# A decoder trunk on one core: key projection by groups of k tiles, norms by two split products, and the last output tiles apart

## The chip, the cores and the metric

The kernel runs on one core of a Trainium2 chip. The metric is the device time of one execution in microseconds. TensorE (PE) multiplies, VectorE (DVE), ScalarE (ACT) and GpSimd (POOL) work on vectors, SyncE (SP) issues nearly all DMAs. Each engine works through its own instructions in the order in which they were written.

## The reference

One sequence of 256 positions, width 2048, float32, two layers. Layer 0 mixes by attention, layer 1 by a gated linear recurrence; each ends with a gated MLP. What bears on the change:

```
h   = x * rsqrt(mean(x*x) + EPS) * gain                    # before every block: 4 norms in all
qkv = h @ w_qkv                                            # 32 query heads, 8 key and 8 value heads of 64
q, k = rmsnorm(q, q_gain), rmsnorm(k, k_gain)              # over the 64 values of a head
S   = q k^T / 8, causal window of 128, softmax with a learned sink, then O = P v
x   = x + O @ w_o
u   = causal_dwconv3(h @ w_up); g, v = split(u)            # 2048 -> 2 x 6144
x   = x + (gelu(g) * v) @ w_down                           # 6144 -> 2048
# layer 1: x = x + (scan(...) * gelu(h @ w_in_y)) @ w_out, and the same MLP
```

## The kernel before

Positions lie along the free dimension (256 columns), channels along the 128 partitions: `x[:, k]` is k tile `k` of 16. To keep float32 accuracy at the speed of the fp32r format, each operand is split into a high part (an fp32r copy, ACT) and a low part (the difference, DVE), and a product is the sum of three: high weights by high and by low data, low weights by high data. A *chunk* is one [128 x 2048] block of weights (1 MB). Chunks come in the order of a list (`order`); `dma_next`, `split_hi` and `split_lo` load one, copy its high part and subtract its low part, each through three buffers; `advance` does one step of all three.

The program is written out by hand, engine by engine (`manual_schedule`): an instruction that waits holds up all that stands behind it on its engine. An SP DMA takes one of eight completion semaphores in turn and waits until the transfer that had it before has landed, so at most eight transfers are under way.

In order: (1) the four key chunks (`psk`; the products `pk`). Chunks 0 and 1 go by quarters, as x and the weights arrive; chunks 2 and 3 follow whole. (2) The values `pv`, four chunks. Between the second and the third of them `kv_norm` (L476) sums x*x over the channels with products by a matrix of ones; the squares were added up by `early_stat` (ACT squares, DVE adds). (3) Sixteen query tiles j: `attend` (L662) spreads the scores `S` of tile j-1, its softmax, and the value products `O` of tile j-3 among the projection of tile j. `k_epi` and `k_fin` (L446, L457) normalise the four key tiles: `k_epi` copies, adds and squares, `k_fin` sums the squares by a product with `bones` (`ks`), takes the root and writes the parts `kz` that the scores read. Key tile 0 is done in stage 2, tiles 1 to 3 start behind query tiles 1, 3 and 7. (4) The output projection, the MLP, the recurrence (`px`, `py`, `pr`) and the second MLP.

At the start of four stages (`pu` twice, `px`, `pr`) stands `late_pair` (L290): two chunks together, with k tiles 14 and 15 last, and between them, except for `pr`, the norm's product `norm_pe` (L181) of two float32 products. The last output tiles are `x_epi`'s (L245): two additions and two DMAs out.

Of the kernel before, what the change touches and what calls it, by code (L numbers as in the profile page):

```python
# [19 lines left out]
F32 = mybir.dt.float32  # L20
# [5 lines left out]
P = 128  # L26
# [14 lines left out]
def trunk(ctx, tc, xT, wq, wk, wv, wo, win, wg, wout, wup, wdn, mixg, ffng, kqg, sinks,  # L41
# [19 lines left out]
    sqt = per.tile([P, 2, T], F32, name="sqt")  # L61
# [3 lines left out]
    vt = per.tile([P, T], F32, name="vt")  # L65
    nt = per.tile([P, T], F32, name="nt")
# [7 lines left out]

    gap.tile([P, 16], F32, name="pad")
# [82 lines left out]
    def stat(src, first):  # L158

        if first:  # L160
            pool.tensor_tensor(out=sqa, in0=src, in1=src, op=ALU.mult)  # L161
        else:
            pool.tensor_tensor(out=sqt, in0=src, in1=src, op=ALU.mult)
            pool.tensor_tensor(out=sqa, in0=sqa, in1=sqt, op=ALU.add)
# [125 lines left out]
    def late_pair(ps, rhs, mid=None):  # L290

        parts = [use(), use()]
        for i, (hi, lo) in enumerate(parts):
            mm_hi(ps[:, i], hi, rhs, rng(0, KD - 2))
            mm_lo(ps[:, i], lo, rhs, rng(0, KD - 2), stop=False)
        advance()
        if mid:
            mid()
        for i, (hi, lo) in enumerate(parts):
            mm_hi(ps[:, i], hi, rhs, rng(KD - 2, KD), start=False)  # L300
            mm_lo(ps[:, i], lo, rhs, rng(KD - 2, KD))
        advance()
# [25 lines left out]
    def quarter(i):  # L328
        return slice(i * CH // 4, (i + 1) * CH // 4)

    def part(i):
        return slice(i * CH // 2, (i + 1) * CH // 2)

    act.dma_start(out=x[:, 0:1, :], in_=xT[:, 0:1, :])
    act.dma_start(out=gm, in_=mixg)
    for c in range(3):
        raws[c] = rawp.tile([P, CH], F32, tag="raw", name=f"raw{c}")
        his[c] = hip.tile([P, CH], F32R, tag="hi", name=f"hi{c}")
        los[c] = lop.tile([P, CH], F32R, tag="lo", name=f"lo{c}")
    for i in range(4):  # L340
        nc.sync.dma_start(out=raws[0][:, quarter(i)], in_=order[0][:, quarter(i)])
        for a, b in ((1, 2), (2, 4)) if i == 0 else ((4 * i, 4 * i + 4),):
            nc.sync.dma_start(out=x[:, a:b, :], in_=xT[:, a:b, :])
        nc.sync.dma_start(out=raws[1][:, quarter(i)], in_=order[1][:, quarter(i)])
    for i in range(2):
# [747 lines left out]
```

## Time and profile before

| | |
|---|---|
| device time, median of 3 | 2152.42 us (2151.99 to 2154.63) |
| the profiled execution | 2152.51 us, span 2150.7 us |
| PE busy | 2144.2 us (100%), 17930 products |
| DVE, ACT, POOL busy | 68%, 52%, 7% |
| DMA | 405.80 MB, mean 189 GB/s |

The busy share of PE is not its peak: products overlap in the array and their ends are modelled. What counts is from start to start, and where PE waits with nothing in flight. A row of the timeline gives the start, the time it covers, engine, source line, operation, output from inputs, shape and count; in brackets stands how long the engine was idle before it and what it waited for. Rows of several instructions are runs of the same kind.

### The profile page before, as it was taken

The numbers are of one execution on the slowest core, as the hardware profiler recorded it, in microseconds if no ns is written. First come the engines' busy times: TensorE is split into PE (matmuls) and PEld (weight loads), VectorE is DVE, ScalarE is ACT, GpSimd is POOL, SyncE is SP. The second block draws the span as 40 slices with busy tenths as digits, with TensorE's granted clock in tenths as the row PEclk, the third lists the DMA queues.
The fourth block names the chain that finished last, engine by engine and source line by source line (L and its number), as shares of the span: only waits on it lengthen the run. The fifth ranks groups of instructions, "written<-read, shape, count | busy, mean of one in ns | idle before, by whom it ended". The sixth has DMA issues, their size and how long they took to land.

```text
span 2150.7 us, 40983 instructions
## 1 busy us (share of the span) xinstructions
PE 2144.2 (100%) x17930; PEld 2104.3 (98%) x17930; DVE 1459.9 (68%) x1715; ACT 1125.7 (52%) x1317; POOL 140.4 (7%) x125
## 2 busy tenths in 40 slices
PE   9999999999999999999999999999999999999999
PEld 7999999999999999999999999999999999999999
DVE  6787867777644777766679877777775447777643
ACT  6676555555433555544479874555553335555432
POOL 1233320000000000002200004100000000000000
PEclk9999999999999999999999999999999999999999
DMA  7333555555555555555555546555555555555453
GB/s 267 115 119 119 216 178 209 192 191 194 194 196 192 200 195 192 191 187 196 177 215 217 187 147 214 187 205 194 192 191 189 196 192 201 195 193 191 181 202 138
DMA packets 60803, 405.80 MB, mean 189 GB/s; under 512 B 7504, under 2 KB 9936, under 8 KB 12880
## 3 DMA queue, kind: packets, MB, share of 16 engines
q1 hardware_dynamic: 60336, 403.04, 52.6%
q8 instruction: 140, 2.29, 0.4%
q14 instruction: 39, 0.32, 0.0%
q10 hardware_dynamic: 288, 0.15, 0.0%
HBM read 401.06 MB, written 2.10 MB: 187 GB/s over the span
## 4 chain that ended last, share of the span: by engine, by line
PE 97%; DVE 1%; DMA 1%; ACT 1%; issue 0%; DVEq 0%; ACTq 0%
PE pu L204 29%; PE pu L209 15%; PE pd L204 14%; PE pd L209 7%; PE pu L250 4%; PE pd L250 3%; PE py L204 3%; PE pq L204 2%; PE po L204 2%; PE px L204 2%; PE pr L204 2%; PE py L209 1%; PE po L209 1%; PE pr L250 1%; PE pq L209 1%; PE px L209 1%
## 5 line engine op out<-in xcount | busy, mean ns | idle before, releaser
L126 DVE TENSOR_TENSOR lo<-raw,hi 128x2048 fp32r<-128x2048 f32 (+1 forms) x390 | 863.8, 2215 | 279.6 <-ACT hi L118 278.2
L118 ACT CAST hi<-raw 128x2048 fp32r<-128x2048 f32 x373 | 713.1, 1912 | 576.1 <-PE pd L204 216.0
L204 PE MATMUL pu<-h,hi 128*128 128x256 f32 x5504 | 651.8, 276 | 0.0
L204 PEld LDWEIGHTS pu<-h,hi 128*128 128x128 f32 x5504 | 636.6, 188 | 0.0
L209 PE MATMUL pu<-h,lo 128*128 128x256 f32 x2752 | 339.9, 276 | 0.0
L204 PE MATMUL pd<-g,hi 128*128 128x256 f32 x2688 | 332.0, 276 | 0.0
L209 PEld LDWEIGHTS pu<-h,lo 128*128 128x128 f32 x2752 | 324.7, 188 | 0.0
L204 PEld LDWEIGHTS pd<-g,hi 128*128 128x128 f32 x2688 | 317.1, 188 | 0.0
L788 DVE SCALAR_TENSOR_TENSOR uy<-us,fw,uy 128x255 f32<-128x255 f32 (+1 forms) x384 | 176.5, 480 | 6.8
L209 PE MATMUL pd<-g,lo 128*128 128x256 f32 x1344 | 179.6, 276 | 0.0
L209 PEld LDWEIGHTS pd<-g,lo 128*128 128x128 f32 x1344 | 164.8, 188 | 0.0
L288 DVE TENSOR_TENSOR us<-pu,rb 128x512 f32<-128x512 f32 x86 | 59.5, 692 | 149.5 <-PE pu L209 149.5
L795 ACT CAST g<-us 128x256 fp32r<-128x256 f32 x96 | 39.0, 407 | 230.3 <-DVE us L794 230.3
L785 ACT ACTIVATE uy<-us,fb,fw 128x256 f32<-128x256 f32 x192 | 105.1, 595 | 55.3 <-DVE us L288 52.6
L204 PE MATMUL pq<-h,hi 128*128 128x256 f32 x512 | 73.9, 284 | 0.0
L796 DVE TENSOR_TENSOR g<-us,g 128x256 fp32r<-128x256 f32 x96 | 40.9, 426 | 45.3 <-ACT g L795 45.3
L260 DVE TENSOR_TENSOR x<-pd,x 128x512 f32<-128x512 f32 (+1 forms) x35 | 19.8, 583 | 70.1 <-PE pd L209 70.1
L204 PEld LDWEIGHTS pq<-h,hi 128*128 128x128 f32 x512 | 64.6, 188 | 0.2
L161 POOL TENSOR_TENSOR sqa<-x 128x512 f32<-128x512 f32 x3 | 5.0, 1671 | 891.1 <-DVE x L260 891.1
L250 PE MATMUL pu<-h,hi 128*128 128x512 f32 (+1 forms) x272 | 61.9, 378 | 0.0
L204 PE MATMUL py<-h,hi 128*128 128x256 f32 x512 | 60.6, 276 | 0.0
L204 PEld LDWEIGHTS py<-h,hi 128*128 128x128 f32 x512 | 59.2, 188 | 0.0
(247 smaller groups left out, 2134.2 us busy)
## 6 DMA issues: line engine op xcount, KB each, us to landing
raw<-in_wup SPq DMA_DIRECT2D x192, 1024.0 KB, 4.8
raw<-in_wdn SPq DMA_DIRECT2D x96, 1024.0 KB, 4.9
raw<-in_win SPq DMA_DIRECT2D x32, 1024.0 KB, 4.9
raw<-in_wq SPq DMA_DIRECT2D x16, 1024.0 KB, 4.8
raw<-in_wo SPq DMA_DIRECT2D x16, 1024.0 KB, 4.8
raw<-in_wout SPq DMA_DIRECT2D x16, 1024.0 KB, 4.8
raw<-in_wv SPq DMA_DIRECT2D x4, 1024.0 KB, 6.2
graw<-in_wg SPq DMA_DIRECT2D x8, 512.0 KB, 3.5
```

Of the source, the lines that this page charges most:

```text
L118: act.copy(out=his[c], in_=raws[c])
L126: dve.tensor_tensor(out=los[c][:, part], in0=raws[c][:, part], in1=f(his[c][:, part]), op=ALU.subtract)
L161: pool.tensor_tensor(out=sqa, in0=src, in1=src, op=ALU.mult)
L204: pe.matmul(ps, lhsT=hi[:, off + k * n:off + k * n + P], rhs=rhs[:, xk, part, :], start=start and (k, part) == (ks[0][0], 0), stop=False)
L209: pe.matmul(ps, lhsT=lo[:, off + k * n:off + k * n + P], rhs=rhs[:, xk, 0, :], start=False, stop=stop and k == ks[-1][0])
L250: pe.matmul(ps[:, cols], lhsT=w, rhs=rhs, start=first, stop=stop and last.get(id(ps)) == i)
L260: dve.tensor_tensor(out=xs[:, i], in0=ps[:, i, 0:T], in1=t[:, i] if two else xs[:, i], op=ALU.add)
L288: dve.tensor_tensor(out=s[:, i], in0=ps[:, i, 0:T], in1=rbb[:, i], op=ALU.mult)
L785: act.activation(out=y[:, i, :], in_=s[:, i, :], func=AF.Identity, scale=fw[:, layer, n, 2:3], bias=fb[:, layer, n:n + 1])
L788: dve.scalar_tensor_tensor(out=y[:, i, tap:], in0=s[:, i, 0:T - tap], scalar=fw[:, layer, n, 2 - tap:3 - tap], in1=y[:, i, tap:], op0=ALU. ...
L795: act.copy(out=g[:, m, 0, :], in_=s[:, 0, :])
L796: dve.tensor_tensor(out=g[:, m, 1, :], in0=s[:, 0, :], in1=f(g[:, m, 0, :]), op=ALU.subtract)
```

## The change

- All four key chunks go side by side through five groups of k tiles (2, 2, 4, 4, 4): per group five DMAs, the splits, and 12 products per k tile. The low data has a product of its own (`two_hi`, 256 columns) instead of sharing one of 512 columns. Chunk 3's parts lie for the time in `kz`.
- `early_stat` and `kv_norm` move later: the norm now stands between the third and fourth chunk of `pv`. Key tile 0 is finished behind query tile 0 instead of in stage 2. The square of a key tile moves from `k_epi` into `k_fin`, just ahead of the product that reads it.
- The norm's sum: DVE folds the two halves of the squares, ACT and DVE split the result, and two fp32r products take the place of two float32 ones.
- `late_pair` becomes `first_pair`: chunk by chunk, the norm behind both.
- The last two output tiles have PSUM tiles of their own, and their additions stand apart.
- The sums of q's squares (`pq`) are issued before the third product of the first score tile; the softmax scaling on POOL goes head by head.

```diff
-    def norm_pe(ps):
+    def norm_sum(ps):
+        dve.tensor_tensor(out=sqa[:, 0], in0=sqa[:, 0], in1=sqa[:, 1], op=ALU.add)
+        act.copy(out=sqt[:, 0], in_=sqa[:, 0])
+        dve.tensor_tensor(out=sqt[:, 1], in0=sqa[:, 0], in1=f(sqt[:, 0]), op=ALU.subtract)
         for i in range(2):
-            pe.matmul(ps, lhsT=ones, rhs=sqa[:, i, :], start=i == 0, stop=i == 1)
+            pe.matmul(ps, lhsT=onesr, rhs=sqt[:, i], start=i == 0, stop=i == 1)
...
-    def late_pair(ps, rhs, mid=None):
+    def first_pair(ps, rhs, mid=None):
+        for i in range(2):
+            hi, lo = use()
+            if i == 0:
+                two_hi(ps[:, 0, 0:T], hi, rhs, rng(0, KD - 2), start=True)
+                one_lo(ps[:, 0, 0:T], lo, rhs, rng(0, KD - 2), stop=False)
+                two_hi(ps[:, 0, 0:T], hi, rhs, rng(KD - 2, KD))
+                one_lo(ps[:, 0, 0:T], lo, rhs, rng(KD - 2, KD))
+            else:
+                thirds(ps[:, 1, 0:T], hi, lo, rhs, rng(0, KD), 0, P, True, True)
+                if mid:
+                    mid()
+            advance()
...
+        groups = [(0, 2), (2, 4), (4, 8), (8, 12), (12, 16)]
+        for a, b in groups:
+            for c in range(4):
+                nc.sync.dma_start(out=kraw[c][:, a * P:b * P], in_=order[c][:, a * P:b * P])
+                if c == 0:
+                    a0 = max(a, 1)
+                    nc.sync.dma_start(out=x[:, a0:b, :], in_=xT[:, a0:b, :])
...
+        for a, b in groups:
+            for c in range(4):
+                sl = slice(a * P, b * P)
+                act.copy(out=khi[c][:, sl], in_=kraw[c][:, sl])
+                dve.tensor_tensor(out=klo[c][:, sl], in0=kraw[c][:, sl], in1=f(khi[c][:, sl]), op=ALU.subtract)
+                if c == 0:
+                    for k in range(a, b):
+                        split_x(h, x[:, k, :], gm[:, 0], k)
+            for c in range(4):
+                two_hi(psk[c], khi[c], h, rng(a, b), start=a == 0)
+                one_lo(psk[c], klo[c], h, rng(a, b), stop=b == KD)
...
         def k_fin(p):
...
+            act.activation(out=r, in_=s, func=AF.Square)
+            pe.matmul(pk[:, 0:T], lhsT=bones, rhs=r, start=True, stop=True)
...
-        k_from, k_to = {1: 1, 3: 2, 7: 3}, (2, 5, 9)
+        k_from, k_to = {1: 1, 3: 2, 7: 3}, (0, 2, 5, 9)
...
+                    if last:
+                        tiles[1] = mm.tile([P, 2, 512], F32, tag="mm", name="pdlast")[:, 1]
...
+                        for i in range(2):
+                            xs = x[:, 14 + i]
+                            dve.tensor_tensor(out=xs, in0=tiles[i][:, 0:T], in1=xs, op=ALU.add)
+                            nc.sync.dma_start(out=out[:, 14 + i], in_=xs)
```

How the order of instructions moves, at three places. On ACT, behind query tile 3 (`es2` closes the softmax of tile 2, `qh3` and `qsq3` read the finished tile, `kr2` belongs to key tile 2), before:

```order
L610 ACTIVATE pr2_960,sm2_961<-S2_930,nm2_957,rr2_946 128x128 x2
L610 ACTIVATE pr2_960,sm2_961<-S2_930,nm2_957,rr2_946 128x256 x2
L617 ACTIVATE es2_1000<-es2_1000 128x4
L558 CAST qh3_1028<-pq_3_897 128x256
L559 ACTIVATE qsq3_1027<-pq_3_897 128x256
L172 ACTIVATE kr2_1033<-kv2_1032 128x256
```

and now:

```order
L591 ACTIVATE pr2_1046,sm2_1047<-S2_1016,nm2_1043,rr2_1032 128x128 x2
L591 ACTIVATE pr2_1046,sm2_1047<-S2_1016,nm2_1043,rr2_1032 128x256 x2
L598 ACTIVATE es2_1086<-es2_1086 128x4
L455 ACTIVATE kr2_1111<-vn_80 128x256
L539 CAST qh3_1117<-pq_3_983 128x256
L540 ACTIVATE qsq3_1116<-pq_3_983 128x256
L173 ACTIVATE kr2_1111<-kv2_1121 128x256
```

The square (L455) now stands between the softmax of tile 2 and the copies of query tile 3; PE's `ks2` product, which reads it, stands as before right behind the last product of query tile 3.

On DVE around the norm in the `pv` stage (`lo6`, `lo8` are low parts of chunks 6 and 8), before:

```order
L441 TENSOR_TENSOR sqa_75<-sqa_75,sq5_458 128x512
L441 TENSOR_TENSOR sqa_75<-sqa_75,sq6_461 128x512
L441 TENSOR_TENSOR sqa_75<-sqa_75,sq7_464 128x512
L126 TENSOR_TENSOR lo6_495<-raw6_366,hi6_456 128x2048
L485 TENSOR_SCALAR cb_148<-pn_497 128x256
```

and now:

```order
L127 TENSOR_TENSOR lo8_606<-raw8_488,hi8_604 128x2048
L439 TENSOR_TENSOR sqa_75<-sqa_75,sq6_608 128x512
L439 TENSOR_TENSOR sqa_75<-sqa_75,sq7_611 128x512
L184 TENSOR_TENSOR sqa_75<-sqa_75 128x256
L186 TENSOR_TENSOR sqt_76<-sqa_75,sqt_76 128x256
L477 TENSOR_SCALAR cb_124<-pn_614 128x256
```

The low part of a chunk now stands ahead of the last two additions and of the norm's own split.

On PE at the start of the recurrence (`px0` is the first pair, `pnr` the norm), before:

```order
L192 MATMUL px0_12050<-h_73,hi184_11966 128x512 x14
L198 MATMUL px0_12050<-h_73,lo184_11968 128x256 x14
L192 MATMUL px0_12050<-h_73,hi185_12020 128x512 x14
L198 MATMUL px0_12050<-h_73,lo185_12022 128x256 x14
L183 MATMUL pnr_12113<-sqa_75,ones_79 128x256 x2
L192 MATMUL px0_12050<-h_73,hi184_11966 128x512 x2
L198 MATMUL px0_12050<-h_73,lo184_11968 128x256 x2
```

and now:

```order
L209 MATMUL px0_12171<-h_73,hi184_12087 128x256 x28
L214 MATMUL px0_12171<-h_73,lo184_12089 128x256 x14
L209 MATMUL px0_12171<-h_73,hi184_12087 128x256 x4
L214 MATMUL px0_12171<-h_73,lo184_12089 128x256 x2
L209 MATMUL px0_12171<-h_73,hi185_12141 128x256 x32
L214 MATMUL px0_12171<-h_73,lo185_12143 128x256 x16
L188 MATMUL pnr_12274<-sqt_76,onesr_88 128x256 x2
```

k tiles 14 and 15 are read after 42 products instead of after 56 longer ones, and the norm comes behind the whole pair.

## Rows read from the trace of the kernel before

**Rows 1.** The page, costliest groups: splits of whole chunks (after the bar: busy, mean ns)
```profile
L126 DVE TENSOR_TENSOR lo<-raw,hi 128x2048 fp32r<-128x2048 f32 (+1 forms) x390 | 863.8, 2215 | 279.6 <-ACT hi L118 278.2
L118 ACT CAST hi<-raw 128x2048 fp32r<-128x2048 f32 x373 | 713.1, 1912 | 576.1 <-PE pd L204 216.0
```

**Rows 2.** Windows: busy us (count) by engine, then PEclk, DMA share, GB/s
```profile
10.00:20.00 10.00, 10.00 (x55) 7.91 (x54) 9.32 (x19) 9.22 (x19) 0.00 (x0) 1.00 1.03 376
400.00:500.00 100.00, 100.00 (x885) 100.00 (x884) 69.73 (x82) 52.37 (x56) 0.00 (x0) 1.00 0.55 193
```

**Rows 3.** Timeline, key stage, PE and DVE: start, us covered, instruction, idle before
```profile
6.27 2.07 PE L192 MATMUL pk<-h,hi 128*128 128x512 f32 x4 [0.65 <-DVE h L155]
...
8.99 1.57 PE L192 MATMUL pk<-h,hi 128*128 128x512 f32 x4
...
14.42 1.29 DVE L406 TENSOR_TENSOR lo<-raw,hi 128x512 fp32r<-128x512 f32 x2
...
26.31 3.95 PE L192 MATMUL pk<-h,hi 128*128 128x512 f32 x16 [0.63 <-ACT hi L118]
...
31.91 0.39 PE L524 MATMUL pv<-hi,h 128*128 128x512 f32 x1
```

**Rows 4.** Transfers issued from 0 to 14 us: count, KB each, median us to landing
```profile
x<-in_xT SPq DMA_DIRECT2D x1, 128.0 KB, 3.7
```

**Rows 5.** Timeline around the norm of the value stage
```profile
40.85 2.29 DVE L441 TENSOR_TENSOR sqa<-sqa,sq 128x512 f32<-128x512 f32 x3 [2.81 <-ACT sq L439]
...
43.19 1.13 PE L183 MATMUL pn<-sqa,ones 128*128 128x256 f32 x4
...
44.96 0.48 PE L524 MATMUL pv<-hi,h 128*128 128x512 f32 x1
```

**Rows 6.** Timeline: key tile 0 finished, then query tile 0 and the first scores
```profile
55.27 0.83 ACT L473 CAST kz<-kst 64x256 fp32r<-64x256 f32 x2 [1.99 <-DVE kst L470]
...
63.22 0.42 DVE L560 TENSOR_TENSOR qh<-pq,qh 128x256 fp32r<-128x256 f32 x1 [2.63 <-ACT qsq L559]
63.86 0.28 PE L575 MATMUL S<-kz,qh 128*128 128x256 f32 x1
```

**Rows 7.** Timeline: the `ks` products behind query tiles 1, 3 and 7, with ACT
```profile
69.81 0.20 ACT L617 ACTIVATE es<-es 128x4 f32<-128x4 f32 x1
69.83 0.59 PE L460 MATMUL ks<-kst,bones 128*128 128x256 f32 x2
...
87.33 0.59 PE L460 MATMUL ks<-sqt,bones 128*128 128x256 f32 x2
89.02 0.21 ACT L617 ACTIVATE es<-es 128x4 f32<-128x4 f32 x1
...
125.08 0.59 PE L460 MATMUL ks<-nt,bones 128*128 128x256 f32 x2
125.68 0.20 ACT L617 ACTIVATE es<-es 128x4 f32<-128x4 f32 x1
```

**Rows 8.** Timeline, PE: the q sums of query tiles 3 to 6, one per tile
```profile
91.17 0.50 PE L580 MATMUL S<-bones,qsq 128*128 128x2 f32 x4
100.98 0.50 PE L580 MATMUL S<-bones,qsq 128*128 128x2 f32 x4
109.98 0.50 PE L580 MATMUL S<-bones,qsq 128*128 128x2 f32 x4
119.38 0.50 PE L580 MATMUL S<-bones,qsq 128*128 128x2 f32 x4
```

**Rows 9.** Timeline, recurrence: first pair, a split behind it, and the next chunk
```profile
1077.37 3.37 PE L192 MATMUL px<-h,hi 128*128 128x512 f32 x14
...
1081.10 2.27 DVE L126 TENSOR_TENSOR lo<-raw,hi 128x2048 fp32r<-128x2048 f32 x1
...
1089.27 3.60 PE L250 MATMUL px<-h,hi 128*128 128x512 f32 x15
```

**Rows 10.** Timeline, DVE: the last two additions
```profile
2147.04 0.76 DVE L260 TENSOR_TENSOR x<-pd,x 128x256 f32<-128x256 f32 x2 [12.99 <-PE pd L209]
```

More of the change, by code (lines that the diff above doesn't have):

```diff
@@ L162, in stat @@
         else:
[L163 to L164 removed]
+            pool.tensor_tensor(out=vn, in0=src, in1=src, op=ALU.mult)
+            pool.tensor_tensor(out=sqa, in0=sqa, in1=vn, op=ALU.add)
     def rsqrt(y, v, tmp):
@@ L325, in rng @@
         return [(k, k) for k in range(a, b)]
[L328 to L332, printed above, removed]
     act.dma_start(out=x[:, 0:1, :], in_=xT[:, 0:1, :])
     act.dma_start(out=gm, in_=mixg)
[L336 to L345, printed above, removed]
-        nc.sync.dma_start(out=raws[2][:, part(i)], in_=order[2][:, part(i)])
-    st["dma"] = 3
     pool.memset(ones, 1.0)
+    pool.tensor_copy(out=onesr, in_=ones)
     act.preload_act_table_set("natural_log_exp_and_others")
@@ L421, in trunk @@
-        st["hi"] = st["lo"] = 3
-        st["use"] = 2
-        for c in range(2):
-            raws.pop(c), his.pop(c), los.pop(c)
-        dma_next()
-        dma_next()
-        for i in range(2):
-            split_part(2, part(i))
-        raws.pop(2)
-        pool.memset(f(kz), 0.0)
-        dve.tensor_tensor(out=kq, in0=kg[:, 0:1], in1=kg[:, 1:2], op=ALU.mult)
-        dve.tensor_scalar(out=kq, in0=kq, scalar1=HD ** -0.5, scalar2=None, op0=ALU.mult)
-        dve.tensor_scalar(out=nsnk, in0=snk, scalar1=-1.0, scalar2=None, op0=ALU.mult)
+        pk01 = psS.tile([P, 2, 512], F32, tag="S", name="pk01")
@@ new lines, in trunk @@
+        psk = [pk01[:, p, 0:T] for p in range(2)]
+        psk += [pj.tile([P, 512], F32, tag="pj", name=f"pk{p}")[:, 0:T] for p in (2, 3)]
+        for a, b in groups:
[9 more added lines that the diff above has]
+                one_lo(psk[c], klo[c], h, rng(a, b), stop=b == KD)
@@ L489, in kv_norm @@
             rsqrt(rc, rcv, rct)
[L491 to L507 removed]
+        for p in range(2):
+            split_hi()
+            split_lo()
+            dma_next()
+            k_epi(p)
+        pool.memset(f(kz), 0.0)
+        dve.tensor_tensor(out=kq, in0=kg[:, 0:1], in1=kg[:, 1:2], op=ALU.mult)
+        dve.tensor_scalar(out=kq, in0=kq, scalar1=HD ** -0.5, scalar2=None, op0=ALU.mult)
+        dve.tensor_scalar(out=nsnk, in0=snk, scalar1=-1.0, scalar2=None, op0=ALU.mult)
         nc.sync.dma_start(out=gf, in_=ffng)
@@ L620, in softmax @@
             dve.reciprocal(out=sm, in_=esf)
-            for b in range(2):
-                for a in range(2):
+            for a in range(2):
+                for b in range(2):
                     i = 2 * b + a
@@ L819, in ffn @@
                     tiles = [ps[:, i] for i in range(2)]
+                    last = half == 1 and nxt is None and dp == 7
+                    if last:
+                        tiles[1] = mm.tile([P, 2, 512], F32, tag="mm", name="pdlast")[:, 1]
                     for c in range(3):
@@ L1025, in trunk @@
             finish(pend)
-            pend = x_epi(ps, 2 * n, 2, gf[:, 1], r2, tag="y", two=n == 0 or two)
+            pend = x_epi(ps, 2 * n, 2, gf[:, 1], r2, tag="y", two=n > 0 and two)
         finish(pend)
```

144 lines of the change are left out of this document (56 added, 88 removed).

## The prediction

> **What bounds the kernel now.** The page comes first: PE is busy for 100% of the span and the chain that ended last is PE for 97%. The windows say what that busy time is worth. In a stretch of the first MLP 885 products start in 100 us, the granted clock stands at 1.00 and every other engine has time over [rows 2]. So one product of 256 columns costs 100/885 = 0.113 us, and a chunk (48 of them) 5.44 us. Most of the kernel runs at this pace before and after, and the change moves none of it. What is left are the places where PE does other work or waits: the first 45 us, the attention, the four stage starts and the last microsecond. The timeline of those places gives every term below.
>
> Times are worked out against the profiled execution, 2152.51 us; the median of the three is 2152.42, so the same sum holds for both within 0.1 us. A measurement of this kernel can tell some 0.2% from no change, which is 4.3 us. A plus below is time gained.
>
> **Key stage: +2.1.** Before, PE starts at 6.27 and the first product of `pv` at 31.91 [rows 3]: 25.64 us for four chunks, of which 4 x 5.44 = 21.8 is the work at the full pace. The rest is a slow start (the first four products of 512 columns cover 2.07 us, 0.52 each, where sixteen later ones cover 3.95, 0.25 each), waits such as the 0.63 us at 26.31, and the products of a quarter that wait for x: the four from 8.99 on cover 1.57 instead of 1.0 [rows 3]. Afterwards there are 192 products of 256 columns, 192 x 0.113 = 21.7. PE should start about 1 us earlier (≈5.3), since a first group is two k tiles instead of four and its copies are half as long. The half pace lasted in the trace to about the row at 8.99; from 5.3 that is 3.7 us, of which half, 1.9, is lost. For waits on x and DVE I allow 0.5: a group of four k tiles costs DVE four subtractions of 0.65 (1.29 for two [rows 3]) and four of x at 0.42 (the 256-column one of [rows 6]), 4.3 us, against PE's 48 products of 5.44, so DVE is ahead once it has started. 5.3 + 21.7 + 1.9 + 0.5 = 29.4. No row shows a chunk that lies in `kz`, or the first `pv` chunk behind this stage's DVE work; I add 0.4, a wait like the 0.63. So `pv` starts at ≈29.8, 2.1 sooner. Bounds: without slow start beyond what is shown and without waits 28.6 (+3.3); with 2.7 us more of waits, three times the wait and slow start that I allow for x, 32.5 (-0.6).
>
> **The norm in the value stage: -0.15.** Before, four float32 products stand between 43.19 and the next product at 44.96 [rows 5]: 1.77 us. The new ones are split products: two sums of two products each take 2 x 0.113, and the small `pc` ones behind them some 0.4 as before. But PE must now wait. On DVE the low part of the fourth value chunk stands ahead of the last two additions, the fold and the difference. That chunk's copy needs a buffer that is free when `pv`'s second chunk is done, ≈11.1 us after `pv` starts. From there: copy 1.9, low part 2.2 [rows 1], two additions at 0.76 (2.29 for three [rows 5]), fold 0.42, copy 0.4, difference 0.42: 18.1 us after the start of `pv`. PE reaches the norm after three chunks and a little, 16.85. Wait 1.25, and 1.25 + 0.65 = 1.9 against 1.77. Bounds: no wait +1.1; a wait of 1.7, -0.6.
>
> **The attention: -3.7.** Three things move here.
> First, key tile 0 is finished behind query tile 0. Before, its `kz` is written from 55.27 on, eight microseconds ahead of the first score product at 63.86, which waits for `qh`'s low part (63.22 + 0.42) alone [rows 6]. Now DVE writes `kst` (0.48, estimated from the 0.42 beside it), ACT copies (0.83/2 for each half) and DVE subtracts (0.42 each), all behind `qh`: 63.64 + 0.48 + 0.42 + 0.44 ≈ 65.05. PE, with nothing else to do there, waits 1.2.
> Second, the squares. A `ks` product reads a square that ACT makes; before, it was made in `k_epi`, long ago. Now it stands in ACT's queue behind the exponentials and `es` of a softmax. Behind query tile 3, `ks` starts at 87.33, while `es` starts at 89.02 and ends at 89.23 [rows 7]. The square ends 0.42 later at 89.65; less 0.25 that the wait of 1.2 above has already given ACT, PE waits 2.05. Behind tile 1, `es` starts at 69.81, `ks` at 69.83 [rows 7]: 0.2 + 0.42 = 0.65. Behind tile 7, 125.68 + 0.2 + 0.42 against 125.08: 1.2, of which I take 1.1. Sum with the first: 5.0.
> Third, what comes back. A period of a query tile is 9.00 us in the steady part (100.98 to 109.98), but 9.81 before that and 9.40 after it [rows 8]: 0.8 and 0.4 are waits on ACT and DVE, which a PE that has just stood still doesn't have. With 0.1 for the rest, 1.3 is returned: -3.7. Issuing the sums of q's squares sooner gains nothing by itself, since the DVE step that reads them also waits for the last score product in the same bank. Bounds: -1.2 (only the first wait stays, ACT ahead elsewhere) to -5.0 (nothing returned).
>
> **The first pairs: +2.5.** Before, the pair of the recurrence runs from 1077.37 to 1089.27 [rows 9], 11.90 us with its norm: 96 products' worth is 10.88, so two float32 products cost about 1. After: 10.88 + 2 x 0.113 = 11.1. That is 0.8 for each of the three pairs with a norm, and 0.15 for the fourth, which has none. The new wait to look for is the earlier use of k tiles 14 and 15: h's last low part is done by 1081.10, where the next thing on DVE starts [rows 9], 3.7 after the pair's start, and it is needed after 42 products, at 4.8. The norm's own chain (a fold, a copy, a difference of 0.4 each) has a whole chunk's time in front of it, and the split of the third chunk, pushed back by that chain and by the norm's place, comes some 0.7 ahead of its use. So no new wait. Bounds: 0.5 of a wait in each, +0.5; at the best +3.0.
>
> **The end: +0.4.** The two last additions are two in a row of 0.38, 0.76 together, behind the last product [rows 10]. Apart, the first one runs while PE still works on tile 15; one is left.
>
> **The sum.** 2.1 - 0.15 - 3.7 + 2.5 + 0.4 = 1.15: 2152.5 - 1.15 = 2151.3. A large count of edits comes out near nothing, because the waits in the attention take back what the starts give.
>
> **The rivals.**
> *ACT gets ahead.* The squares wait only as long as ACT is late with the softmax. At tile 1 ACT is late by 0.2 us, at tile 3 by 1.9 [rows 7]; if the first wait of 1.2 lets ACT and DVE catch up, the squares cost little: attention -1.2 to 0, and 2147.6 to 2148.8. For it speaks that PE's standing still gives the other engines time; against it that 1.2 is less than 1.9, and that the next two periods refill the lag.
> *The small pieces are slow.* The first two groups come as pieces of 128 KB. One such took 3.7 us [rows 4]; eight under way are 8 x 131 KB / 3.7 us = 283 GB/s, against the 376 GB/s of 10 to 20 us [rows 2]. If the key stage's 6.3 MB came at 283, it would be in after 22.2 us of transfer instead of 16.7; with 4.5 us before the flow starts, that is 26.7, and the last group's splits and 48 products end near 33. That is 3.2 later than forecast: 2154.5. Against it: only 2 of the 6.3 MB are in such pieces, and later pieces are 256 KB.
> The Trainium skill, page "DMA: Bandwidth & Descriptors", section "Measured (HBM→SBUF, 128 partitions, SWDGE, issued from GpSimd)", asks for batches of 1 MiB or more for 75% of the peak and lists 138 GB/s at 64 KB and 341 at 1 MB; by it this rival would be the likeliest. The trace disagrees: in the stretch of 10 to 20 us, when quarters of chunks (256 KB) came in, the flow was 376 GB/s [rows 2], with eight under way at once, and so it gets a small chance.
> *The other side: PE falls back to its start pace.* The first products ran at half pace [rows 3]. If each of the four new waits (1.25, 1.2, 2.05, 1.1 us) brought that back for as long as at the start, 6.27 to 8.99 [rows 3], each would cost half of 2.7 more, 1.36: 5.4 in all, 2156.7. It decides from the first wait of over 1 us in which PE's queue is empty. Against it: the wait of 0.63 before the sixteen products at 26.31 left them at the full 0.25 each [rows 3].
> *The change doesn't do what it says.* A chunk in `kz` or the split norm could be no faster than what they replace: without 2.1 and 2.5 but with the waits returned for the most part, 2152.3.
>
> **How the numbers follow.** Forecast 2151.3, own range 2149.8 to 2152.8: 0.50. ACT ahead, 2148.2: 0.20. Slow pieces, 2154.5: 0.13. Half pace, 2156.7: 0.09. Nothing delivered, 2152.3: 0.08. The range takes in the first rival's lower end and the slow pieces: 2147.8 to 2154.4. Faster by over 0.2% means under 2148.1; of ACT ahead about half lies there, and of the forecast a tail where the key stage is at its best: 0.18. Slower by over 0.2% is above 2156.7, most of the half-pace case and a tail of the slow pieces: 0.06. The rest, 0.76, can't be told from no change.
>
> **What would show it.** The first `pv` product at ≈29.8 (33 if the pieces are slow). PE idle for ≈1.25 ahead of the norm in the `pv` stage, released by DVE or ACT. PE idle for ≈1.2 ahead of the first score product, released by `kz`. PE idle ahead of the three `ks` products for 0.65, 2.05 and 1.1, released by ACT's square; the forecast is wrong if these are absent. Pairs of 11.1 us at px0 and the two `pu`; a wait of PE at k tile 14 or at the third chunk would refute that term. A last DVE addition of 0.38 alone. The products behind each wait at 0.113 a piece refute the half pace.

## The result and the profile after

The changed kernel takes 2157.58 us (median of 15 runs, 2154.61 to 2159.79), the kernel before, run beside it, 2154.36 (2151.99 to 2156.6 but for one run far off). The ratio is 1.0016, 95% interval 1.001 to 1.0023: slower by 0.16%, where 2151.3 was forecast. The profiled execution took 2156.59 us with a span of 2154.7, 4.0 more than before. Read at the starts of the stages, the two traces differ so:

| stage (PE, start to start) | before | after | gained |
|---|---|---|---|
| key stage: to the first `pv` product | 31.91 | 32.60 | -0.7 |
| value stage: to the first `pq` product | 24.76 | 25.59 | -0.8 |
| attention: to the first `po` product | 141.08 | 146.72 | -5.6 |
| output projection: to the first `pu` product | 94.60 | 95.05 | -0.45 |
| four first pairs | | | +3.03 |
| the end | | | +0.58 |

The starts and the end gave a little more than forecast; the first three stages took more than they should, and the output projection, for which nothing was forecast, 0.45 more. Where PE waits, the view of the waits says (line, what it waited for, total, times, longest):

```profile
PE ks L456 <- ACT kr L455: 2.7, 3, 1.4
PE pk L209 <- ACT h L155: 2.7, 2, 2.1
PE S L556 <- DVE kz L468: 1.0, 1, 1.0
PE idle L411 <- POOL ones L336: 1.0, 1, 1.0
PE pn L188 <- ACT sqt L185: 0.9, 1, 0.9
PE pq L209 <- DVE kv L459: 0.5, 1, 0.5
```

Four of them stand in the prediction (`ks`, `S`, `pn`, and a small one of `pk`). Two do not: 2.1 us in the key stage, and 0.5 at the first query tile.

**Key stage.** The timeline of PE shows a hole behind the two first groups, which were done by 11.6 us, then products at twice their price (`pv` aside, all rows are `pk`):

```profile
13.73 2.36 PE L209 MATMUL pk<-h,hi 128*128 128x256 f32 x8 [2.14 <-ACT h L155]
15.89 1.05 PE L214 MATMUL pk<-h,lo 128*128 128x256 f32 x4
...
21.57 1.07 PE L209 MATMUL pk<-h,hi 128*128 128x256 f32 x8
...
31.17 1.12 PE L209 MATMUL pk<-h,kz 128*128 128x256 f32 x8
...
32.60 0.40 PE L507 MATMUL pv<-hi,h 128*128 128x512 f32 x1
```

ACT, which PE waits for, waits itself for a piece of chunk 0 and then for x:

```profile
11.91 0.62 ACT L419 CAST hi<-kraw 128x512 fp32r<-128x512 f32 x1 [2.70 <-DMA kraw<-in_wk]
13.17 1.71 ACT L155 ACTIVATE h<-x,gm 128x256 fp32r<-128x256 f32 x4 [0.65 <-DMA x<-in_xT]
```

The windows of 5 us (the last three columns are PEclk, DMA share, GB/s) show both the cause and what followed:

```profile
5.00:10.00 5.00, 4.69 (x36) 4.39 (x37) 4.12 (x11) 3.56 (x11) 0.30 (x1) 1.00 0.82 234
10.00:15.00 5.00, 2.73 (x18) 2.23 (x18) 1.98 (x5) 2.44 (x6) 0.00 (x0) 0.96 0.98 338
15.00:20.00 5.00, 5.00 (x32) 5.00 (x32) 4.98 (x10) 4.91 (x11) 0.00 (x0) 0.70 1.04 406
20.00:25.00 5.00, 5.00 (x46) 5.00 (x45) 5.00 (x11) 4.08 (x9) 0.00 (x0) 1.00 1.04 415
```

From 5 to 10 us the flow is 234 GB/s, not the 376 of [rows 2] (240 to 272 in six more executions of the same stage, below); and the granted clock is 0.96 and 0.70 on average in the two windows in which the wait ends and the work goes on. Time at the lower level (1.2 of 2.4 GHz) is twice what is missing from 1: 0.04 x 5 x 2 + 0.30 x 5 x 2 = 3.4 us, of which half, 1.7, is lost. The last rows also show that eight products whose weights lie in `kz` take 1.12, those of the other three chunks 1.07.

**Norm.** It went as forecast. DVE's rows of the chain, one behind the other:

```profile
45.72 2.29 DVE L127 TENSOR_TENSOR lo<-raw,hi 128x2048 fp32r<-128x2048 f32 x1 [0.91 <-ACT hi L119]
47.93 1.48 DVE L439 TENSOR_TENSOR sqa<-sqa,sq 128x512 f32<-128x512 f32 x2
49.44 0.42 DVE L184 TENSOR_TENSOR sqa<-sqa 128x256 f32<-128x256 f32 x1
50.34 0.43 DVE L186 TENSOR_TENSOR sqt<-sqa,sqt 128x256 fp32r<-128x256 f32 x1 [0.47 <-ACT sqt L185]
```

PE starts the norm at 50.45 after 0.87 of idling and goes on with the fourth chunk at 51.40, 2.0 us after the end of the third chunk, against 1.77 in [rows 5]. The other 0.5 of this stage is a wait for the PSUM bank of query tile 0: it holds the `ks` product of key tile 0 until DVE has read it, which is only now finished behind the values.

**Attention.** Behind query tile 3 ACT and PE stand as forecast (ACT's square directly behind `es`, PE's `ks` released by it):

```profile
92.23 0.21 ACT L598 ACTIVATE es<-es 128x4 f32<-128x4 f32 x1
92.34 0.40 ACT L455 ACTIVATE kr<-vn 128x256 f32<-128x256 f32 x1
```

```profile
92.79 0.70 PE L456 MATMUL ks<-kr,bones 128*128 128x256 f32 x2 [1.42 <-ACT kr L455]
```

1.42 instead of 2.05; tiles 1 and 7 give 0.38 and 0.92 instead of 0.65 and 1.1, the first score 1.01 instead of 1.2. As idle time that is 3.7 where 5.0 was forecast, but idle time is not the whole price of a wait: it is counted only from the modelled end of the last product (0.28 us after its start, where the next one would start after 0.113), so that each of these waits costs 0.2 to 0.4 us more from start to start (e2 and e8 below). Of the 2 us that the stage lost beyond the forecast a good part lies in rows without a wait, the low products of a query tile late in the stage:

```profile
148.10 2.04 PE L214 MATMUL pq<-h,lo 128*128 128x256 f32 x16
157.28 1.98 PE L214 MATMUL pq<-h,lo 128*128 128x256 f32 x16
166.34 2.05 PE L214 MATMUL pq<-h,lo 128*128 128x256 f32 x16
```

Sixteen products cover 1.98 us (0.1133 apart) or 2.05 (0.1178). Before, all query tiles from the third on have 1.98. A period of a query tile is now 9.21 to 9.24 us in three late tiles of four and 9.00 in the fourth, where it was 9.00 in nearly all of them before, and nothing waits in it.

**First pairs and the end.** The pair of the recurrence, to be set beside [rows 9]:

```profile
1084.01 3.34 PE L209 MATMUL px<-h,hi 128*128 128x256 f32 x28
...
1094.89 0.39 PE L188 MATMUL pnr<-sqt,onesr 128*128 128x256 f32 x2
1095.12 1.07 PE L255 MATMUL px<-h,hi 128*128 128x512 f32 x4
```

11.11 us instead of 11.90. From the pair's start to the next stage's start 0.96 us is gained in each of the three with a norm, 0.15 in the fourth; PE waits in none of them. At the end one addition is left behind the last product, beside [rows 10]:

```profile
2148.88 0.42 DVE L816 TENSOR_TENSOR x<-pd,x 128x256 f32<-128x256 f32 x1 [10.27 <-PE pd L214]
2151.60 0.42 DVE L816 TENSOR_TENSOR x<-pdlast,x 128x256 f32<-128x256 f32 x1 [2.29 <-PE pdlast L214]
```

### The profile page after: what moved, and what is told of

Same layout as the page of the kernel before. It is cut to its first block, busy times and chain, and to the rows that moved or that the text cites. A ratio compares the mean times of both kernels' runs of the same rounds, so it can differ in the third digit from the quotient of the medians.

```text
span 2154.7 us, 41359 instructions
## 1 busy us (share of the span) xinstructions
PE 2142.2 (99%) x18106; PEld 2110.8 (98%) x18106; DVE 1457.5 (68%) x1724; ACT 1126.5 (52%) x1327; POOL 141.0 (7%) x126
## 4 chain that ended last, share of the span: by engine, by line
PE 97%; ACT 1%; DVE 1%; DMA 0%; issue 0%; SPq 0%; ACTq 0%; DVEq 0%
PE pu L209 30%; PE pu L214 15%; PE pd L209 14%; PE pd L214 7%; PE pu L255 4%; PE pd L255 3%; PE py L209 3%; PE px L209 2%; PE pq L209 2%; PE po L209 2%; PE pr L209 2%; PE py L214 1%; PE po L214 1%; PE px L214 1%; PE pq L214 1%; PE pr L255 1%
## 5 line engine op out<-in xcount | busy, mean ns | idle before, releaser
L209 PE MATMUL pu<-h,hi 128*128 128x256 f32 x5632 | 667.2, 276 | 0.0
L209 PEld LDWEIGHTS pu<-h,hi 128*128 128x128 f32 x5632 | 651.6, 188 | 0.0
L214 PE MATMUL pu<-h,lo 128*128 128x256 f32 x2816 | 348.1, 276 | 0.0
L214 PEld LDWEIGHTS pu<-h,lo 128*128 128x128 f32 x2816 | 332.4, 188 | 0.0
L209 PE MATMUL pd<-g,hi 128*128 128x256 f32 x2640 | 326.0, 276 | 0.0
L209 PEld LDWEIGHTS pd<-g,hi 128*128 128x128 f32 x2640 | 311.5, 188 | 0.0
L255 PEld LDWEIGHTS pu<-h,hi 128*128 128x128 f32 x272 | 47.8, 188 | 8.5
```

The costliest lines, as they stand in the source:

```text
L209: pe.matmul(ps, lhsT=hi[:, off + k * n:off + k * n + P], rhs=rhs[:, xk, part, :], start=start and (k, part) == (ks[0][0], 0), stop=False)
L214: pe.matmul(ps, lhsT=lo[:, off + k * n:off + k * n + P], rhs=rhs[:, xk, 0, :], start=False, stop=stop and k == ks[-1][0])
L255: pe.matmul(ps[:, cols], lhsT=w, rhs=rhs, start=first, stop=stop and last.get(id(ps)) == i)
```

## The experiments

Theories: (a) the key stage lost by late transfers and by the clock that fell behind them; (b) the waits of the attention are what the squares and key tile 0 cost; (c) the order of the small products sets the pace of the large ones. Rivals: the clock falls anyway; ACT and DVE give the waits back elsewhere; the pace belongs to memory or to chance. Ratios are to the kernel before on the same chip.

How far a single execution can be trusted differs by stage. The attention of the changed kernel took 146.6 to 146.8 us in five executions that don't differ in it (the changed kernel twice, e3, e4, e5), so differences there of half a microsecond count. Its key stage is less steady: in the five executions that don't differ in it (the changed kernel twice, e1, e2, e8) `pv` starts anywhere from 30.98 to 33.08. The whole time differs by up to 2.7 us with the pace of products in the output projection. The intervals of e1, e3 and e5 overlap that of the changed kernel (1.001 to 1.0023), so for these the stage times carry the argument and the medians don't. When a transfer landed is read from the trace of the execution in question.

**Sums of q's squares in their old place** (`e1_sums_back`)

```diff
-                if kk[0] == 0:
+                pe.matmul(o, lhsT=ql[:, 1, tb], rhs=kz[:, p, 0, kk[0], kk[1]], start=False, stop=True)
+                if kk[0] == 1:
                     for c in range(2):
                         pe.matmul(pq[:, 2 * c:2 * c + 2], ...
-                pe.matmul(o, lhsT=ql[:, 1, tb], rhs=kz[:, p, 0, kk[0], kk[1]], start=False, stop=True)
```

> The changed kernel with one thing undone: the sums of q's squares stand again behind the third product of the second score tile. If the order of PE's instructions within a query tile holds the products at 0.118 us a piece instead of 0.113, the steady periods return from 9.22 to 9.00 us, the output projection starts 2.0 to 2.5 us sooner than in the changed kernel (204.9) and the whole takes about 2.2 us less (2154.3 or so). Rival: the pace comes from where the tiles lie in memory or from the stalls; then periods stay at 9.22 and the time within 0.4 us of the changed kernel's.

The steady periods are 9.00 again, and the attention takes 145.14 us instead of 146.72: 1.6 less, where 2.0 to 2.5 were expected. This is (c). The whole gained nothing in the profile (span 2155.5), against the 2.2 expected: the pace of 0.1178 took hold behind the attention and lasted to 317 us, so the output projection took 96.9 us instead of 95.05. Median 2156.36, ratio 1.0011 (1.0002 to 1.002). The low products of a tile:

```profile
147.28 1.98 PE L214 MATMUL pq<-h,lo 128*128 128x256 f32 x16
```

The waits are all still there, and with the old order the q sums of tiles 2 to 4 can be set beside [rows 8] (the first row here is tile 2 in the kernel before):

```profile
81.62 0.50 PE L580 MATMUL S<-bones,qsq 128*128 128x2 f32 x4
...
85.18 0.50 PE L561 MATMUL S<-bones,qsq 128*128 128x2 f32 x4
96.66 0.50 PE L561 MATMUL S<-bones,qsq 128*128 128x2 f32 x4
105.66 0.50 PE L561 MATMUL S<-bones,qsq 128*128 128x2 f32 x4
```

The period with the `ks` wait of tile 3 (1.54 idle) is 11.48 where it was 9.56, and the next one is 9.00 where it was 9.81; the one of 9.40 is 9.00 too. Those 1.2 us are what the waits give back: in b1 below, with the old order and without the waits, the two are 9.71 and 9.41 again.

**The same part alone, in the kernel before** (`e7_before_sums_sooner`)

```diff
-                pe.matmul(o, lhsT=ql[:, 1, tb], rhs=kz[:, p, 0, kk[0], kk[1]], start=False, stop=True)
-                if kk[0] == 1:
+                if kk[0] == 0:
                     for c in range(2):
                         pe.matmul(pq[:, 2 * c:2 * c + 2], ...
+                pe.matmul(o, lhsT=ql[:, 1, tb], rhs=kz[:, p, 0, kk[0], kk[1]], start=False, stop=True)
```

> The kernel before with one part of the change alone: the sums of q's squares ahead of the third product of the first score tile. If their place sets the pace, the steady periods of a query tile go from 9.00 to about 9.2 us here too, most products of the attention stand 0.118 apart, and the output projection starts 1.5 to 2.5 us later than 197.75. Rival: the pace came from the other parts (memory, waits), and the periods stay at 9.00.

```profile
142.85 2.05 PE L209 MATMUL pq<-h,lo 128*128 128x256 f32 x16
```

The periods go from 9.00 to 9.21 to 9.28 in most tiles; attention 142.21 instead of 141.08, +1.1. The output projection starts 1.9 later than 197.75, as expected, but 0.8 of it is from the key stage, where no edit is. The two periods that were longer before, 9.81 and 9.40, are 9.26 and 9.23, so they gain where the others lose. Median 2154.22, ratio 1.0008 (0.9999 to 1.0017). No other part of the change and no new address is in it, so the order alone does it.

**Squares early** (`e2_squares_early`)

```diff
+            if p < 2:
+                ksq[p] = ks["t"][:, 2, p]
+                act.activation(out=ksq[p], in_=ks[p], func=AF.Square)
...
-            act.activation(out=r, in_=s, func=AF.Square)
-            pe.matmul(pk[:, 0:T], lhsT=bones, rhs=r, start=True, stop=True)
+            pe.matmul(pk[:, 0:T], lhsT=bones, rhs=ksq.pop(p), start=True, stop=True)
...
                 kv_norm()
+                for p in (2, 3):
+                    ksq[p] = sqa[:, p - 2]
+                    act.activation(out=ksq[p], in_=ks[p], func=AF.Square)
```

> The changed kernel with the squares of the key tiles made early again (0 and 1 right behind their copies, 2 and 3 behind the norm of the value stage), each in a place of its own. If the three waits of the ks products (0.38, 1.42, 0.92) come from ACT's queue, they go, and the output projection starts 2.0 to 2.7 us sooner than 204.9; the wait ahead of the first score product (1.0) stays. Rival: ACT and DVE are late anyway and the waits turn up at the transposes or the value products behind; then less than 0.8 us is gained.

The three waits are gone, the one ahead of the first score stands:

```profile
67.61 0.39 PE L561 MATMUL S<-kz,qh 128*128 128x256 f32 x1 [1.02 <-DVE kz L470]
73.70 0.59 PE L458 MATMUL ks<-kst,bones 128*128 128x256 f32 x2
91.52 0.59 PE L458 MATMUL ks<-sqa,bones 128*128 128x256 f32 x2
```

The attention took 143.43, 3.3 us less, for 2.7 of idle time: the three periods are 0.64, 1.70 and 1.09 shorter than in the changed kernel, where PE was idle for 0.38, 1.42 and 0.92. In the key stage this execution had a longer wait than the changed kernel's (2.72 us, `pv` at 33.08), which the profiled run's 2154.08 has in it. Median 2152.72, ratio 1.0002 (0.9993 to 1.0011).

**Squares early, and key tile 0 finished in the value stage** (`e8_k0_early`: the edit of e2, and on top of it)

```diff
                     act.activation(out=ksq[p], in_=ks[p], func=AF.Square)
-        fin = k_fin(0)
-        step(fin)
-        step(fin)
+                fin = k_fin(0)
+                step(fin)
+            if c == 3:
+                finish(fin)
...
-        k_from, k_to = {1: 1, 3: 2, 7: 3}, (0, 2, 5, 9)
+        k_from, k_to = {1: 1, 3: 2, 7: 3}, (2, 5, 9)
...
```

> The version with early squares, and key tile 0 finished in the value stage as in the kernel before. The wait of 1.0 us ahead of the first score product and the one of 0.5 us at the start of query tile 0 should go; less what ACT and DVE, now with 1.5 us less lead, make PE wait behind. Between the start of query tile 0 and the output projection 143.4 us in the version with early squares: 142.4 here if all of the first wait is gained, 143.2 if it is given back.

Attention 142.03, 1.4 less than in e2 for 1.0 of idle time, and no wait ahead of the first query tile or the first score. Median 2152.72, ratio 0.9996 (0.9987 to 1.0005); the profile has the slow pace through the output projection (97.3 us).

**The wait of the key stage filled** (`e3_fill_wait`)

```diff
+            if a == 4:
+                for i in range(8):
+                    pe.matmul(idle[:, 0:P], lhsT=ones, rhs=ones, start=True, stop=True)
             for c in range(4):
                 two_hi(psk[c], khi[c], h, rng(a, b), start=a == 0)
```

> The changed kernel with 8 products of ones by ones more (16 passes of 128 columns) between the second and third group of the key stage, where PE waits for 2.14 us. If the half pace of 13.7 to 18 us is a price of that wait, the clock stays at its upper level, and the value products start about 1.7 us sooner (half of the 3.4 us at the lower level): 30.9 instead of 32.6. Rival: the clock falls whatever PE does there, or the data are late for the following groups too; then they start at 32.6 or later.

```profile
11.37 1.95 PE L426 MATMUL idle<-ones 128*128 128x128 f32 x16
13.22 2.10 PE L209 MATMUL pk<-h,hi 128*128 128x256 f32 x8
15.16 0.63 PE L214 MATMUL pk<-h,lo 128*128 128x256 f32 x4
```

The windows from 5 to 25 us all show a granted clock of 1.00, and the four low products take 0.63 instead of 1.05. `pv` starts at 30.93, 1.67 sooner. The number expected was met in part by luck: 0.5 of it is that x landed sooner in this execution (12.64 instead of 13.15, so that the third group starts at 13.22 instead of 13.73), and 1.16 is the time from there to `pv`, 17.71 instead of 18.87. That is (a): in the three executions in which the wait stood unfilled and the clock fell behind it (the changed kernel, e1, e2) this time is 18.7 to 19.3, with the wait filled or absent (here, e6, e8) 17.6 to 17.9. Median 2155.28, ratio 1.0011 (1.0002 to 1.0021).

**x's first k tiles asked for by ACT** (`e4_x_by_act`)

```diff
+    act.dma_start(out=x[:, 1:4, :], in_=xT[:, 1:4, :])
     act.preload_act_table_set("natural_log_exp_and_others")
+    act.dma_start(out=x[:, 4:8, :], in_=xT[:, 4:8, :])
...
-                if c == 0:
-                    a0 = max(a, 1)
-                    nc.sync.dma_start(out=x[:, a0:b, :], in_=xT[:, a0:b, :])
+                if c == 0 and a >= 8:
+                    nc.sync.dma_start(out=x[:, a:b, :], in_=xT[:, a:b, :])
```

> The changed kernel with x's k tiles 1 to 7 asked for by ACT's queue at the start (two transfers), instead of SP's behind the key pieces. If the wait of 2.14 us at the third group comes from SP's queue (one transfer after another, eight under way), it goes, the clock doesn't fall, and the value products start at 28.5 to 29.5: 3 to 4 us less. Rival: pieces of 128 KB are slow in themselves and the sum of the transfers is the limit; then the wait moves to a key piece and the value products start at 32 or later.

Neither came out as written. The wait at the third group is gone (its x landed at 10.36 instead of 13.15), but ACT's row for the second k tile shows a wait for x, not for a key piece, at the front,

```profile
7.51 0.51 ACT L155 ACTIVATE h<-x,gm 128x256 fp32r<-128x256 f32 x1 [2.06 <-DMA x<-in_xT]
```

the clock fell behind it (at 8.06), and `pv` starts at 31.84, neither 28.5 to 29.5 nor 32 or later. So when x is asked for matters, but sooner isn't free: the key pieces asked for at the same time took longer (the third chunk's first piece landed at 7.29 instead of 5.04), which speaks for a limit on what is under way. It doesn't show it alone, since x's k tiles 1 to 3 are one transfer of 384 KB here where the changed kernel has one of 128 KB for k tile 1. Median 2158.3, ratio 1.0025 (1.0015 to 1.0035), part of it the slow pace, which lasted to 318 us here.

**Groups of four** (`e5_groups_of_4`)

```diff
-        groups = [(0, 2), (2, 4), (4, 8), (8, 12), (12, 16)]
+        groups = [(0, 4), (4, 8), (8, 12), (12, 16)]
```

> The changed kernel with four groups of four k tiles in the key stage: 16 key pieces of 256 KB instead of 8 of 128 KB and 12 of 256 KB. If the small first pieces make the third group late (one issue per 0.45 us, 8 under way), the flow from 4 to 12 us rises from 200-310 towards 376 GB/s, the wait of 2.14 us and the clock's fall go, and the value products start at 29.5 to 31 although PE begins later (6 to 7 instead of 5.2). Rival: the transfers are as slow with 256 KB, the wait moves to the start of the first and second group, and the value products start at 32 or later.

```profile
6.32 2.33 PE L209 MATMUL pk<-h,hi 128*128 128x256 f32 x8 [1.80 <-ACT h L155]
8.45 1.05 PE L214 MATMUL pk<-h,lo 128*128 128x256 f32 x4
9.30 1.85 PE L209 MATMUL pk<-h,hi 128*128 128x256 f32 x8
10.99 0.63 PE L214 MATMUL pk<-h,lo 128*128 128x256 f32 x4
```

One wait of 1.80 ahead of the first group, none later in the key stage; `pv` starts at 30.86. PE begins 1.1 us later than in the changed kernel and is through 1.7 sooner. x's k tiles 4 to 7 land at 9.70 instead of 13.15, and the flow from 4 to 12 us is 383 GB/s instead of 245. Half pace lasts until about 11 us (granted clock 0.75 and 0.90 in the windows from 5 to 15). The norm's wait is 1.70 here instead of 0.87, so of the gain half is lost again in the value stage (26.41). Median 2156.0, ratio 1.0013 (1.0004 to 1.0022): the profile has the slow pace to 318 us, and the output projection took 97.3.

**The changed kernel again** (`e6_after_again`, no edit)

> The changed kernel again, for a second profile. If the pace of 0.118 us a product is a state that PE keeps until something breaks the row, and into which it falls by chance of some hundredths of a microsecond, then the same program shows another share of slow products (886 in the first profile, 1047 and 1482 in two variants that change nothing after the attention), and its time differs by 0.0045 us for each. Rival: the pace belongs to the program; then the counts agree within some tens.

2156.48 us, span 2154.6, with 811 slow products in the place of 886 (256 columns, the next of the same kind 0.116 to 0.120 us behind): neither some tens nor the hundreds that (c) with chance allows, so how much is chance stays open. But the second profile lost its time elsewhere: in the key stage there was no wait at the third group; PE ran at half pace to 10.3 us, and `pv` started at 30.98. The data weren't sooner by much: x's k tiles 4 to 7, which the third group needs, landed at 12.80 instead of 13.15. PE was later (its third group starts at 13.39), so the half pace at the start took up the time that the other execution spent waiting. Then the norm's wait of 1.23 us came, and behind it the clock fell in the value stage:

```profile
50.00:55.00 5.00, 5.00 (x17) 3.99 (x17) 1.42 (x7) 2.51 (x4) 0.00 (x0) 0.66 0.18 74
55.00:60.00 5.00, 4.48 (x26) 3.60 (x25) 1.98 (x4) 1.52 (x3) 0.00 (x0) 1.00 0.00 0
```

0.34 x 5 x 2 = 3.4 us at the lower level again, 1.7 lost. Of the new waits the one in the value stage can have the price that the third rival named; those of the attention had it in no profile.

**All waits met** (`b1_all_fixed`; the edits of e1, e2, e8 and e3 together, and this one; `kv_norm` calls the `split_lo` handed to it behind `norm_sum`)

```diff
             if c < 3:
-                split_lo()
+                if c < 2:
+                    split_lo()
                 early_stat(*((0, 1, 2), (3, 4, 5), (6, 7))[c])
...
-                kv_norm()
+                kv_norm(split_lo)
...
```

> The changed kernel with all new waits met: squares early, key tile 0 finished in the value stage, sums of q's squares in their old place, 8 products of ones in the key stage's wait, and on DVE the low part of the next chunk behind the norm's own split instead of ahead of it. From the runs so far against the changed kernel: waits -2.7, first score -1.0, its buffer wait -0.5, pace -1.6, clock -1.7, norm -0.9: 8.4 less than 2154.7 in the span, 2146.3, and a time of 2148; 2151.5 if the slow pace lasts to the end of the output projection. Rival: ACT and DVE give the waits back at the transposes and value products; then 2150 to 2152.

Span 2146.4, median 2147.97, ratio 0.9978 (0.9968 to 0.9987): the sum of 2146.3 came out, and the norm waits for nothing. Stage by stage it came out in part by luck. Against the changed kernel the key stage gave 0.9 (1.7 in the sum), the value stage 1.6 (1.4), the attention 5.3 (5.3, though e2, e8 and e1 apart had gained 6.3: with the old order the two long periods come back), the output projection 0.5, which the sum didn't have. In the key stage there was hardly a wait to fill here, since PE was done with the second group only when x had landed (12.92), and the filling itself was in the way:

```profile
13.19 1.95 PE L426 MATMUL idle<-ones 128*128 128x128 f32 x16
14.90 1.19 PE L209 MATMUL pk<-h,hi 128*128 128x256 f32 x8
```

The third group starts at 14.90, where it started at 13.1 to 13.4 in the two executions without a wait (e6, e8), and `pv` at 31.70 instead of 31.0.

**The same with groups of four** (`b2_fixed_groups4`)

```diff
-        groups = [(0, 2), (2, 4), (4, 8), (8, 12), (12, 16)]
+        groups = [(0, 4), (4, 8), (8, 12), (12, 16)]
...
-            if a == 4:
-                for i in range(8):
-                    pe.matmul(idle[:, 0:P], lhsT=ones, rhs=ones, start=True, stop=True)
```

> As the version with all waits met, but with groups of four k tiles in place of the filled wait. If groups of four cost no wait, the value products start at 29.5 to 31 and it is within 1 us of the other; if the transfers are the limit they start at 32 or later and it is 1 to 3 us slower than the other.

`pv` at 30.63, 1.1 sooner than in the other; median 2147.55, ratio 0.9973 (0.9963 to 0.9983): within 1 us of the other.

**A longer warm-up** (`b3_longer_warmup`: b2 with 12 products of ones at the start)

```diff
-        for i in range(8):
+        for i in range(12):
             pe.matmul(idle[:, 0:P], lhsT=ones, rhs=ones, start=True, stop=True)
```

> The version with all waits met and groups of four, with 12 instead of 8 products of ones at the start, so that PE works until the first data are there (6.3 us instead of a wait of 1.6 us). If the half pace up to 10.3 us comes from that wait, the value products start 1 to 1.8 us sooner than 30.6, and the time falls to 2146 to 2146.7. Rival: the half pace belongs to the start whatever PE does there, and nothing changes.

```profile
0.99 5.14 PE L411 MATMUL idle<-ones 128*128 128x128 f32 x24 [0.99 <-POOL ones L336]
6.30 2.10 PE L209 MATMUL pk<-h,hi 128*128 128x256 f32 x8 [0.17 <-ACT h L155]
8.24 0.62 PE L214 MATMUL pk<-h,lo 128*128 128x256 f32 x4
8.69 1.07 PE L209 MATMUL pk<-h,hi 128*128 128x256 f32 x8
```

The data of the first group come at the same time, 6.30, but the four low products take 0.62 instead of the 1.05 of groups of four without it. `pv` starts at 29.41, 1.2 sooner, behind the first microsecond no wait over 0.33 us is left, and the median is 2146.16, ratio 0.997 (0.9958 to 0.9981): faster than both kernels. Its profile has the slow pace from 208 to 308 us and is of the slowest of its six runs (2148.91; the others 2146.10 to 2146.42).

## Why the prediction was wrong

Forecast -1.15, measured +4.0 in the span: 5.1 us apart.

- *Key stage, +2.1 forecast, -0.7 measured: the step that failed most.* The term "for waits on x and DVE I allow 0.5" was worked out from DVE's load; the flow came in only where the rival was set aside, at the 376 GB/s of a later stretch. PE was idle for 0.55 us ahead of the first group and for 2.14, waiting for x, ahead of the third. In the changed kernel the flow from 5 to 10 us was 234 GB/s, and with groups of four and 256 KB pieces (b3) in the same window 368. x's k tiles 4 to 7 landed at 12.3 to 13.8 us in all seven executions of these groups, and the third group can't start sooner. The rule of the Trainium skill, page "DMA: Bandwidth & Descriptors", section "Measured (HBM→SBUF, 128 partitions, SWDGE, issued from GpSimd)", which asks for large batches, had been set aside; the flows of 234 and 368 agree with its direction, though with 256 KB pieces PE no longer waited behind the first group (e5, b3). The second part is the clock: 3.4 us at the lower level behind the wait, 1.7 lost by the granted clock, 1.2 by the starts in e3. The half-pace term at the start (1.9) was the wrong one for this profile: there the products were at full pace by 6.5 us. In the second profile of the same program it was right, and the stage gained 0.9 (e6).
- *The rival of the small pieces*, held at 0.13, had the number of this stage right (33 against 32.6), by luck: it had the flow at 283 GB/s throughout, where the windows from 10 to 25 us show 338 to 415, and part of what made up the 33 in the run was the clock, which it doesn't name.
- *Value stage, -0.15 forecast, -0.8 measured.* The norm's 1.25 of waiting came out as 0.87 idle, its 1.9 in all as 2.0. Missed was the bank of the `ks` product that query tile 0 waits for, 0.5. In the second profile, where the clock fell here instead, the stage lost 2.7. Taken together the key and the value stage end 3.5 and 3.75 us later than forecast in the two profiles.
- *Attention, -3.7 forecast, -5.6 measured.* The mechanism of the waits was right, all four stand where they were named, and so was their size. Without the three `ks` waits the stage is 3.3 us shorter (e2), without the one ahead of the first score another 1.4 (e8); with the sums in their old place all of them together are worth 3.7 (145.14 in e1, 141.40 in b1). The 1.3 to be returned came too: 1.2 in e1. What failed is the sentence that the sooner sums gain "nothing by itself", a term put at nothing. They cost 0.6 to 1.6 us (1.6 from the changed kernel to e1, 1.1 from the kernel before to e7, 0.6 between e8 and b1): they break the row of products at another place, and PE goes on at 0.1178 instead of 0.1133.
- *Output projection, nothing forecast, -0.45 measured.* The slow pace runs on into it: 180 slow products there, 81 before.
- *First pairs +2.5 and end +0.4*: 3.03 and 0.58. Mechanism and size were right, no new wait came.
- *The half-pace rival* (four times 1.36, 2156.7) lies nearest to the measured 2157.58, but by luck: it was right that such a wait can pull the clock down, wrong that each does. There was one fall of 3.4 us, 1.7 lost by the granted clock, in each of the two profiles of the changed kernel.
- Two sums of the prediction are slightly off, without weight for the result: the chain of the norm adds up to 18.0 and not 18.1, and the key stage without waits to 28.9 and not 28.6.

How the slow pace is spread: 559 slow products in the profile before, 886 and 811 in two of the changed kernel, 1482, 1483 and 1542 in e4, e5 and e8, where it lasted through the output projection (97.3 us instead of 94.6 to 95.05; in e1 and b3 96.9). At 0.0045 us each that is 2.7 us between profiles that differ in nothing behind the key stage (the changed kernel, e4, e5). Whether it is also why the runs of one kernel spread as they do (2154.6 to 2159.8 for the changed one) wasn't shown; that b3's one profile, with it, took 2.5 to 2.8 us more than its five other runs would fit.

## What to carry to other kernels

When PE is busy all the time, a change is worth what it does to waits, to the clock behind a wait, and to the pace of products in rows where nothing waits; compare that pace (sixteen products, 1.98 or 2.05 us) before looking for a stall. A flow measured in the steady part isn't the flow of the start: size the first pieces by the flow in their own window, and keep PE at work until the first data are there. A filling for a wait that comes in one execution and not in another costs its own length where the wait stays out (b1). Idle time in the waits view is less than what a wait costs; compare starts. An operation whose result a product reads belongs where its engine has nothing queued, not just ahead of the product.

## What the runs showed of the hardware that wasn't expected

- PE has two paces for the same product of 256 columns, 0.1133 and 0.1178 us, at a granted clock of 1.00. Mostly it keeps one until something breaks the row (sums of two columns, transpositions, a wait) and can fall into the other there. Directly behind the sums it was the slow one in both orders (0.118 on average from there to the transpositions, in each of 14 query tiles of the changed kernel, of e1, of e7 and of the kernel before). Behind the transpositions the order told: with the sums ahead of the third product the low products went on slow in 11 of these 14 tiles (the changed kernel) and in 12 (e7), with the sums in their old place they were fast in 13 (e1) and in all 14 (before, b1). What in the engine does this stays open.
- Eight products whose weights lie in `kz` took 1.11 or 1.12 us in the last three groups of the key stage, those of the other chunks 1.07 in the last two groups and 1.10 in the third. Whether that is the address wasn't tried.
- A wait of 2.14 us, and in another execution one of 1.23, were followed by 3.4 us at half clock that began about 1 us after the work had gone on (14.6 after 13.73; about 51.3 after 49.19 and 50.14). In e1, e2, e4 and e5 the same 3.4 us followed waits of 1.34, 2.72, 1.67 and 1.80, 0 to 2.4 us after the work had gone on. The waits of 1.4 us in the attention weren't followed by it, nor were the norm's of 1.35 in e1 and 1.70 in e5. Why some are and others not stays open.
- The key stage of one and the same program waited 2.14 us for x in one execution and hardly at all in another (e6), though x landed nearly at the same time (13.15 and 12.80): in the second PE's first products were slow and hid the wait. What decides whether they are slow (full pace by 6.5 us or half pace to 10.3, at a granted clock of 1.00 in both records) stays open; products of ones up to the first data (b3) made them fast.
